# An RWKV-7 chunk recurrence: the inverse multiplied into keys and query products ahead of a two-product chain

## The chip, the cores and the metric

The kernel runs as one program on one core of a Trainium2 chip. The metric is the device time of one execution in microseconds. In the profile the engines are PE (TensorE, matrix products), PEld (its weight loads), DVE (VectorE), ACT (ScalarE), POOL (GpSimd) and SP (SyncE, which issues the DMAs).

## The reference

One block of a streaming encoder with 1024 tokens of 1024 channels: stick-breaking attention and RWKV-7 time mixing run as parallel branches and are merged by gates; a SwiGLU FFN follows. The change lies in the time mixing, whose recurrence is this (8 heads of 64 channels; `state` is one 64x64 matrix for each head):

```python
def wkv7_scan(r, decay, k, v, kk, a):
    ...
    def step(state, inp):
        r_t, w_t, k_t, v_t, kk_t, a_t = inp
        sa = jnp.einsum('bhvk,bhk->bhv', state, -kk_t)
        state = (state * w_t[:, :, None, :]
                 + sa[..., None] * (kk_t * a_t)[:, :, None, :]
                 + v_t[..., None] * k_t[:, :, None, :])
        return state, jnp.einsum('bhvk,bhk->bhv', state, r_t)
    ...
    _, y = lax.scan(chunk_step, state0, tuple(to_chunks(t) for t in (r, decay, k, v, kk, a)))
    return y.reshape(S, B, H, N).transpose(1, 0, 2, 3)
```

All inputs and outputs are float32.

## The kernel before

The kernel first records all operations of the whole block as a list and then orders them: `Block.schedule` plays them through with a cost for each instruction, latencies between engines, a priority (the place in the list plus an offset) and a limited number of buffers for each class of tiles, and `Block.issue` issues every engine's instructions in the order found. Every instruction therefore stands at line 528 of the profile, and instructions are told apart by the names of their tiles. Each engine executes its instructions in that fixed order. A group written under `b.together()` stays in one piece on TensorE.

The time mixing treats heads in four pairs (`PAIRS`), tokens in two halves of 512 (`hf`), and each half in eight chunks of 64 tokens. The two heads of a pair lie on partitions 0 to 63 and 64 to 127. A pair and a half make a unit, eight units in all.

- `rwkv` goes over the pairs: projections of the next pair (`project`, tile class d, 128x512 matmuls), the elementwise work of the two units, gate projections as filler (`gate_tiles`, also class d, 4, 0, 2 and 6 tiles at the four pairs), and the chain of chunks with the highest priority (`CHAIN`).
- `rw_elementwise` prepares for each unit the decayed keys and queries (`xh`, one array per head: the removal key in columns 0 to 63 and the query in 64 to 127 of each chunk), the right operands `bk`, their transposes `bkt` (the keys the state update needs), the values `sv`, centred by a product with a constant 128x128 matrix, and the products of `bk` and `xh`, masked to the triangles within a chunk. The masked products of a head with itself go into `na`, those of the values into the free half of `xh`. Four mask multiplications on VectorE run for each half of four chunks.
- `rw_inverse` inverts the 64x64 triangular matrix of every chunk and head: the 32x32 diagonal blocks by elimination on VectorE (`q` tiles, after a turn through DRAM as `nd` and `td`), then the block below the diagonal by two products of 32x32 tiles on TensorE (names y<-q,na and y<-q,q in the trace). The inverse replaces the masked product in columns 0 to 63 of `na`.
- `rw_chain` steps through the chunks. Each step consists of three groups of products with copies between them:
  1. px: the state and values in `sv` times the removal keys (c<-sv,xa and c<-sv,xb), and with it the state's part of the outputs `y` (y<-xa,sv and y<-xb,sv). VectorE copies px to `xe`.
  2. pu: the inverse times `xe` (c<-xe,na). VectorE copies head 0, ScalarE head 1 into `sv`.
  3. ps: `bkt` times `sv` (c<-sv,bkt), and with it the rest of the outputs (y<-na,sv). Two scalar_tensor_tensor on VectorE, one for each head, form the next state from ps and from the decayed old state `sp`, which GpSimd makes.

  The last chunk of a pair has no ps. Products of single heads are 64 columns wide and are packed: the two heads use different parts of TensorE's array.
- `rw_post` normalizes `y` and stores it.

After the time mixing come `attention`, `merge`, `output` and `ffn`, which the change does not touch.

Of the kernel before, what the change touches and what calls it, by code (L numbers as in the profile page):

```python
# [590 lines left out]
def hybrid_block(tc, x, w_in, consts, params, rows, ups, gup, w_sb, w_rw, w_o, w_fg, w_fu, w_fd, out):  # L591
# [3 lines left out]
    with ExitStack() as es:  # L595
# [9 lines left out]
        b.cls("xe", 3, CH)  # L605
# [207 lines left out]
def rw_elementwise(b, u, p, hf, spill):  # L813
# [76 lines left out]
    for h, q, rs, qs in quads:  # L890
        nc.sync.dma_start(nd[:, 2 * h + q].rearrange("c s t -> s c t"), na[rs, :, qs])
# [13 lines left out]


# [8 lines left out]
    with Offset(b, INV):  # L915
        rw_inverse(b, nd, na, quads, tinit, p, hf)


def rw_inverse(b, nd, na, quads, tinit, p, hf):
# [26 lines left out]
    with b.together():  # L946
        for c, h in ((c, h) for c in range(8) for h in range(2)):
            nc.tensor.matmul(ph[bot[h], c, :], lhsT=na[top[h], c, 32:CH], rhs=dn[top[h], c, :], start=True, stop=True)
    for h in range(2):
# [4 lines left out]
    with b.together():
        for c, h in ((c, h) for c in range(8) for h in range(2)):
            nc.tensor.matmul(pt[top[h], c, :], lhsT=hb[bot[h], c, :], rhs=dt[bot[h], c, :], start=True, stop=True)
    for h in range(2):
        nc.scalar.copy(na[top[h], :, 32:CH], pt[top[h]])


def rw_chain(b, units, p, hf):
# [4 lines left out]
    y = T("y", [P, H])
    u["y"] = y
    hs = [(0, slice(0, CH)), (1, slice(CH, P))]
    for c in range(8):
# [3 lines left out]
        with b.together():
            for h, rs in hs:
                nc.tensor.matmul(px[rs, :], lhsT=xh[h][:, c, 0:CH], rhs=sv[:, c, rs], start=True, stop=True)
            for h, rs in hs:
                nc.tensor.matmul(y[rs, ys], lhsT=sv[:, c, rs], rhs=xh[h][:, c, CH:P], start=c == 0, stop=False, skip_group_check=True)
# [6 lines left out]
        pu = T("c", [P, CH])
        with b.together():
            for h, rs in hs:
                nc.tensor.matmul(pu[rs, :], lhsT=na[rs, c, 0:CH], rhs=xe[rs, :], start=True, stop=True)
        nc.vector.tensor_copy(sv[hs[0][1], c, hs[0][1]], pu[hs[0][1], :])
        nc.scalar.copy(sv[hs[1][1], c, hs[1][1]], pu[hs[1][1], :])
        ps = None if last else T("c", [P, CH])  # L990
        with b.together():
            if not last:
                for h, rs in hs:
                    nc.tensor.matmul(ps[rs, :], lhsT=bkt[:, c, rs], rhs=sv[:, c, rs], start=True, stop=True)
            for h, rs in hs:
                nc.tensor.matmul(y[rs, ys], lhsT=sv[rs, c, rs], rhs=na[rs, c, CH:P], start=False, stop=c == 7, skip_group_check=True)
# [548 lines left out]
```

## Time and profile before

| | us |
|---|---|
| median of 3 runs (1706.15 to 1707.61) | 1707.52 |
| the profiled execution, its own time | 1704.82 |
| span of its instructions | 1702.7 |
| granted TensorE clock, mean | 0.993 |
| TensorE counted busy in the span | 1641.2 |
| VectorE counted busy in the span | 1212.8 |

The first px of the chain starts at 116.6 us, the chain proper at 183.3 (first pu), and its last products at 578.0. In the rows of the prediction an operation stands as out<-in by the names of the tiles: `c_c<-xe_xe,b_na` is a product that writes a tile of class c from xe and na. The number after the names is the part of the array in rows*columns, then the size of the moving operand. In a timeline the first two numbers are the start and the duration in us. In a table by stretch of time each column is the busy time of PE, PEld, DVE, ACT and POOL in the stretch, with the number of instructions, then the granted clock, the share of the DMA engines and GB/s.

### The profile page before, as it was taken

What the parts mean: (1) busy time and instruction counts of PE and PEld (TensorE: products, weight loads), DVE (VectorE), ACT (ScalarE), POOL (GpSimd) and SP (SyncE); (2) the same over time, 40 slices, a digit from 0 to 9 for tenths busy, and PEclk for the clock granted to TensorE, in tenths of its full rate; (3) what the DMA queues carried; (4) which work ended last, traced back from release to release, by engine and by line L of the source; (5) the groups of instructions that cost most, each with busy time, mean ns of one, the idle gap of its engine ahead of it and who ended that gap; (6) DMA issues with size and microseconds to landing.
All of it is one profiled execution on the core that took longest, in us unless ns stands there. A gap on an engine that the chain in (4) does not pass through costs nothing.

```text
span 1702.7 us, 23795 instructions
## 1 busy us (share of the span) xinstructions
PE 1641.2 (96%) x8868; PEld 1267.2 (74%) x8868; DVE 1212.8 (71%) x2167; ACT 712.5 (42%) x1371; POOL 211.1 (12%) x376
## 2 busy tenths in 40 slices
PE   6999999899999989999999999999999999999998
PEld 5777666566666677777778788888888888888886
DVE  6567688989785598898826644866667666777484
ACT  7522233123223476677644443433223233454352
POOL 2031233323313100000003311000000000000000
PEclk9999999899999999999999999999999999999999
DMA  6522222123221000000253721223232333684355
GB/s 228 186 72 94 64 76 82 40 77 101 81 73 57 32 26 13 26 25 26 91 188 106 255 78 44 87 93 118 82 104 93 118 101 105 238 317 136 125 166 180
DMA packets 98147, 178.85 MB, mean 105 GB/s; under 512 B 33392, under 2 KB 34544, under 8 KB 98032
## 3 DMA queue, kind: packets, MB, share of 16 engines
q1 hardware_dynamic: 98032, 177.34, 31.5%
q8 instruction: 70, 1.15, 0.3%
q14 instruction: 45, 0.37, 0.1%
HBM read 129.86 MB, written 47.45 MB: 104 GB/s over the span
## 4 chain that ended last, share of the span: by engine, by line
PE 76%; DVE 17%; ACT 3%; issue 2%; DMA 1%; SPq 0%; DVEq 0%; POOL 0%; ACTq 0%
PE d_d L528 35%; PE e_e L528 16%; PE c_c L528 16%; PE y_y L528 9%; DVE q_q L528 4%; DVE b_nb L528 3%; DVE b_be L528 2%; DVE b_wt L528 1%; DVE wlo_wlo L528 1%; DVE b_na L528 1%; DVE b_bk L528 1%; DVE b_tmp L528 1%; ACT whi_whi L528 0%; DVE b_xb L528 0%; DVE b_xa L528 0%
## 5 line engine op out<-in xcount | busy, mean ns | idle before, releaser
L528 PE MATMUL d_d<-big_h,whi_whi 128*128 128x512 f32 x1280 | 444.1, 413 | 1.9 <-ACT b_sh L528 1.1
L528 PEld LDWEIGHTS d_d<-big_h,whi_whi 128*128 128x128 f32 x1280 | 235.6, 189 | 55.3 <-issue 5.1
L528 PE MATMUL d_d<-big_h,wlo_wlo 128*128 128x512 f32 x640 | 263.4, 412 | 0.0
L528 PEld LDWEIGHTS d_d<-big_h,wlo_wlo 128*128 128x128 f32 x640 | 120.8, 189 | 25.6 <-issue 1.9
L528 ACT CAST whi_whi<-raw_raw 128x1024 fp32r<-128x1024 f32 (+1 forms) x60 | 55.9, 934 | 99.8 <-PE d_d L528 92.5
L528 DVE TENSOR_TENSOR q_q<-b_nl,q_q 128x2 f32<-128x2 f32 (+30 forms) x248 | 86.7, 350 | 9.2 <-PE y_y L528 2.8
L528 DVE TENSOR_TENSOR wlo_wlo<-raw_raw,whi_whi 128x1024 fp32r<-128x1024 f32 (+1 forms) x60 | 70.4, 1175 | 31.0 <-ACT whi_whi L528 30.6
L528 ACT COPY b_sv<-c_c 64x64 f32<-64x64 f32 x64 | 13.3, 207 | 173.6 <-DVE b_sv L528 114.4
L528 DVE TENSOR_TENSOR_SCAN b_nb<-b_nb 128x128 f32<-128x128 f32 (+3 forms) x64 | 85.5, 1352 | 0.6 <-ACT b_nb L528 0.4
L528 POOL TENSOR_SCALAR sp_sp<-b_sv,pl_pl 64x64 f32<-64x64 f32 x120 | 60.2, 502 | 182.3 <-DVE b_sv L528 176.8
L528 DVE TENSOR_REDUCE q_q<-q_q 128x1 f32<-128x2 f32 (+30 forms) x248 | 62.2, 251 | 6.9
L528 PE MATMUL e_e<-b_wd,big_act 128*128 128x512 f32 x264 | 66.6, 395 | 0.0
L528 PE MATMUL d_d<-b_wd,big_act 128*128 128x512 f32 x264 | 66.6, 394 | 0.0
L528 ACT CAST b_wd<-b_wraw 128x512 fp32r<-128x512 f32 x71 | 42.2, 619 | 53.1 <-DVE b_wraw L528 20.7
L528 DVE TENSOR_TENSOR b_wd<-b_wraw,b_wd 128x512 fp32r<-128x512 f32 x71 | 46.7, 686 | 22.8 <-ACT b_wd L528 22.8
L528 PE MATMUL c_c<-cst_cst,b_be 128*128 128x128 f32 x288 | 46.1, 280 | 17.2 <-DVE b_wt L528 11.4
L528 PEld LDWEIGHTS e_e<-b_wd,big_act 128*128 128x128 f32 x264 | 49.6, 188 | 11.8
L528 PEld LDWEIGHTS d_d<-b_wd,big_act 128*128 128x128 f32 x264 | 49.6, 188 | 11.8
L528 PEld LDWEIGHTS c_c<-cst_cst,b_be 128*128 128x128 f32 x288 | 32.1, 140 | 32.3 <-DVE b_wt L528 17.7
L528 ACT CAST b_wt<-c_c 128x512 fp32r<-128x512 f32 (+2 forms) x96 | 43.8, 482 | 21.1 <-PE c_c L528 19.3
L528 DVE TENSOR_TENSOR b_wt<-c_c,b_wt 128x512 fp32r<-128x512 f32 (+2 forms) x96 | 50.1, 547 | 3.2 <-ACT b_wt L528 2.4
L528 PE MATMUL y_y<-b_wd,big_act 128*128 128x512 f32 x198 | 50.5, 394 | 0.0
(609 smaller groups left out, 3742.9 us busy)
## 6 DMA issues: line engine op xcount, KB each, us to landing
raw_raw<-w_in SPq DMA_DIRECT2D x42, 512.0 KB, 3.4
raw_raw<-w_fg SPq DMA_DIRECT2D x22, 512.0 KB, 3.5
raw_raw<-w_fu SPq DMA_DIRECT2D x22, 512.0 KB, 4.1
b_wraw<-w_fd SPq DMA_DIRECT2D x22, 512.0 KB, 5.1
act<-b_u SPq DMA_DIRECT2D x40, 256.0 KB, 3.4
b_x<-x SPq DMA_DIRECT2D x16, 512.0 KB, 6.0
b_mg<-gsc SPq DMA_DIRECT2D x28, 256.0 KB, 5.2
raw_araw<-act SPq DMA_DIRECT2D x14, 512.0 KB, 4.1
```

Source lines behind the costliest of these rows:

```text
L528: getattr(getattr(self.real, op.engine), op.method)(**kw)
```

## The change

The keys and query products that use the inverse are multiplied with it once for each unit, ahead of the chain, so that a step needs no product with the inverse. A step then is one product of the whole 128x128 `sv` with the keys of both heads (`nx`), two copies, and one product of `bkt` with the result `xv`, again for both heads at once. `xv` is a second array beside `sv`, whose value parts come by DMA. The outputs are no longer made in the steps but for four chunks at a time. A unit holds `ar`, `nx` (two tiles), `sv`, `xv`, `bkt` and the half tile `tt`, where it had `xa`, `xb`, `na`, `sv` and `bkt`. The mask multiplications now take all 128 partitions at once.

```diff
@@ rw_elementwise
-    xh = [T("b", [P, 8, P], F32, "xa"), T("b", [P, 8, P], F32, "xb")]
+    ar = T("b", [P, 8, P], F32, "ar")
     bk = T("b", [P, 8 * P], F32, "bk").rearrange("p (c a t) -> p c a t", c=8, a=2)
-    for h, rs in enumerate(halves):
-        nc.vector.scalar_tensor_tensor(out=xh[h][rs, :, 0:CH], in0=c8(kk)[rs], scalar=-1.0, in1=pp[rs, :, 0:CH], op0=ALU.mult, op1=ALU.mult)
-        nc.gpsimd.tensor_tensor(out=xh[h][rs, :, CH:P], in0=c8(r)[rs], in1=pp[rs, :, 1 : CH + 1], op=ALU.mult)
+    nc.vector.scalar_tensor_tensor(out=ar[:, :, 0:CH], in0=c8(kk), scalar=-1.0, in1=pp[:, :, 0:CH], op0=ALU.mult, op1=ALU.mult)
+    nc.gpsimd.tensor_tensor(out=ar[:, :, CH:P], in0=c8(r), in1=pp[:, :, 1 : CH + 1], op=ALU.mult)
...
-        for h, rs in enumerate(halves):
-            for os in halves:
-                dst = na if os is rs else xh[h]
-                nc.vector.tensor_tensor(out=dst[os, c0 : c0 + 4, :], in0=pts[h][os], in1=mask_a[os, None, :].broadcast_to([CH, 4, P]), op=ALU.mult)
+        for h in range(2):
+            nc.vector.tensor_tensor(out=nx[g][:, :, :, h, :], in0=pts[h].rearrange("p c (a t) -> p c a t", a=2), in1=mask2[:, None].broadcast_to([P, 4, 2, CH]), op=ALU.mult)
...
-        nc.sync.dma_start(nd[:, 2 * h + q].rearrange("c s t -> s c t"), na[rs, :, qs])
+        for g in range(2):
+            nc.sync.dma_start(nd[4 * g : 4 * g + 4, 2 * h + q].rearrange("c s t -> s c t"), nx[g][rs, :, 0, h, qs])
...
+    xv = T("b", [P, 8, P], F32, "xv")
+    nc.sync.dma_start(xv[hi, :, lo], sv[hi, :, lo])
+    nc.sync.dma_start(xv[lo, :, hi], sv[lo, :, hi])
...
     with Offset(b, INV):
-        rw_inverse(b, nd, na, quads, tinit, p, hf)
+        tt = rw_inverse(b, nd, nx, quads, tinit, p, hf)
+        for g in range(2):
+            pt = T("y", [P, 4, P])
+            cs = slice(4 * g, 4 * g + 4)
+            with b.together():
+                for c in range(4):
+                    for h, rs in enumerate(halves):
+                        nc.tensor.matmul(pt[rs, c, 0:CH], lhsT=tt[rs, 4 * g + c, :], rhs=bkt[rs, 4 * g + c, rs], start=True, stop=True)
+                    for h, rs in enumerate(halves):
+                        nc.tensor.matmul(pt[rs, c, CH:P], lhsT=tt[rs, 4 * g + c, :], rhs=nx[g][rs, c, 1, h, :], start=True, stop=True)
+            for h, rs in enumerate(halves):
+                nc.scalar.copy(bkt[rs, cs, rs], pt[rs, :, 0:CH])
+                nc.scalar.copy(nx[g][rs, :, 1, h, :], pt[rs, :, CH:P])
+                nc.scalar.copy(nx[g][rs, :, 0, h, :], ar[rs, cs, 0:CH])
@@ rw_chain
-        px = T("c", [P, CH])
...
+        px = T("c", [P, P])
+        nc.tensor.matmul(px, lhsT=nx[c // 4][:, c % 4, 0].rearrange("p h t -> p (h t)"), rhs=sv[:, c, :], start=True, stop=True)
...
...
-        nc.vector.tensor_copy(xe[:], px[:])
...
+        nc.vector.tensor_copy(xv[r0, c, r0], px[r0, r0])
+        nc.scalar.copy(xv[r1, c, r1], px[r1, r1])
         if not last:
+            ps = T("c", [P, P])
+            nc.tensor.matmul(ps, lhsT=bkt[:, c, :], rhs=xv[:, c, :], start=True, stop=True)
...
+        if c % 4 == 3:
...
+            with b.together():
+                for k in range(4 * g, c + 1):
+                    for h, rs in hs:
+                        nc.tensor.matmul(y[rs, k * CH : k * CH + CH], lhsT=sv[rs, k, rs], rhs=ar[rs, k, CH:P], start=k == 0, stop=False, skip_group_check=True)
+                for k in range(4 * g, c + 1):
+                    for h, rs in hs:
+                        nc.tensor.matmul(y[rs, k * CH : k * CH + CH], lhsT=xv[:, k, rs], rhs=nx[g][:, k % 4, 1, h, :], start=False, stop=k == 7, skip_group_check=True)
```

How this moves TensorE's instructions is seen at three places. The first is a chunk step of pair 0 (d is the filler, c the chain, y the outputs). Before, from the second head of px, with the outputs that go along, to pu:

```order
L528 MATMUL c_c_1624<-b_sv_890,b_xb_800 64x64
L528 MATMUL y_y_1053<-b_xa_793,b_sv_890 64x64
L528 MATMUL y_y_1053<-b_xb_800,b_sv_890 64x64
L528 MATMUL d_d_1599<-big_h_169,wlo_wlo_1486 128x512
L528 MATMUL d_d_1599<-big_h_169,whi_whi_1478 128x512
L528 MATMUL d_d_1599<-big_h_175,whi_whi_1478 128x512
L528 MATMUL d_d_1599<-big_h_169,wlo_wlo_1486 128x512
L528 MATMUL d_d_1599<-big_h_169,whi_whi_1478 128x512
L528 MATMUL d_d_1599<-big_h_175,whi_whi_1478 128x512
L528 MATMUL c_c_1644<-xe_xe_1635,b_na_1036 64x64 x2
```

The same place now, from one px to the next:

```order
L528 MATMUL c_c_1652<-b_sv_885,b_nx_1026 128x128
L528 MATMUL d_d_1632<-big_h_169,whi_whi_1407 128x512
L528 MATMUL d_d_1632<-big_h_175,whi_whi_1407 128x512
L528 MATMUL d_d_1632<-big_h_169,wlo_wlo_1415 128x512
L528 MATMUL d_d_1632<-big_h_169,whi_whi_1407 128x512
L528 MATMUL c_c_1665<-b_xv_930,b_bkt_1072 128x128
L528 MATMUL d_d_1632<-big_h_175,whi_whi_1407 128x512
L528 MATMUL d_d_1632<-big_h_169,wlo_wlo_1415 128x512
L528 MATMUL d_d_1632<-big_h_186,whi_whi_1407 128x512
L528 MATMUL d_d_1632<-big_h_195,whi_whi_1407 128x512
L528 MATMUL d_d_1632<-big_h_186,wlo_wlo_1415 128x512
L528 MATMUL c_c_1680<-b_sv_885,b_nx_1026 128x128
```

A step has two single products with four and five filler matmuls behind them, where it had three groups (the third, ps with its outputs, follows after three more filler matmuls).

The second place is new: behind the fourth chunk of the same unit the outputs of four chunks stand in one bundle.

```order
L528 MATMUL c_c_1692<-b_xv_930,b_bkt_1072 128x128
L528 MATMUL y_y_1695<-b_ar_793,b_sv_885 64x64 x8
L528 MATMUL y_y_1695<-b_nx_1026,b_xv_930 64x64 x8
L528 MATMUL d_d_1632<-big_h_195,whi_whi_1407 128x512
L528 MATMUL d_d_1632<-big_h_186,wlo_wlo_1415 128x512
L528 MATMUL c_c_1722<-b_sv_885,b_nx_1054 128x128
```

They stood in each step before.

The third place is the end of the first half of pair 1. Before, steps follow there with no filler between their groups:

```order
L528 MATMUL y_y_2512<-b_xb_1096,b_sv_1900 64x64
L528 MATMUL c_c_2958<-xe_xe_2955,b_na_1967 64x64 x2
L528 MATMUL c_c_2965<-b_sv_1900,b_bkt_2057 64x64 x2
L528 MATMUL y_y_2512<-b_na_1967,b_sv_1900 64x64 x2
L528 MATMUL c_c_2976<-b_sv_1900,b_xa_1085 64x64
L528 MATMUL c_c_2976<-b_sv_1900,b_xb_1096 64x64
L528 MATMUL y_y_2512<-b_xa_1085,b_sv_1900 64x64
L528 MATMUL y_y_2512<-b_xb_1096,b_sv_1900 64x64
L528 MATMUL c_c_2986<-xe_xe_2983,b_na_1967 64x64 x2
```

Now, in the same half, filler stands between them:

```order
L528 MATMUL c_c_2967<-b_sv_1753,b_nx_1901 128x128
L528 MATMUL d_d_2853<-big_h_186,wlo_wlo_2599 128x512
L528 MATMUL d_d_2853<-big_h_186,whi_whi_2572 128x512
L528 MATMUL d_d_2853<-big_h_195,whi_whi_2572 128x512
L528 MATMUL d_d_2853<-big_h_186,wlo_wlo_2599 128x512
L528 MATMUL c_c_2978<-b_xv_1858,b_bkt_1917 128x128
L528 MATMUL d_d_2853<-big_h_186,whi_whi_2572 128x512
L528 MATMUL d_d_2853<-big_h_195,whi_whi_2572 128x512
L528 MATMUL d_d_2853<-big_h_186,wlo_wlo_2599 128x512
L528 MATMUL d_d_2986<-big_h_169,whi_whi_2756 128x512
L528 MATMUL d_d_2986<-big_h_175,whi_whi_2756 128x512
L528 MATMUL c_c_2993<-b_sv_1753,b_nx_1901 128x128
```

The filler of that place stood further behind before, after the products of the next unit.

More of the change, by code (lines that the diff above doesn't have):

```diff
@@ L604, in hybrid_block @@
         b.cls("bf", 2, P)
-        b.cls("xe", 3, CH)
         b.cls("sp", 3, CH)
@@ L871, in rw_elementwise @@
     u["bv"] = bv
-    na = T("b", [P, 8, P], F32, "na")
-    for c0 in (0, 4):
+    mask2 = mask_a.rearrange("p (a t) -> p a t", a=2)
+    nx = [T("b", [P, 4, 2, 2, CH], F32, "nx") for g in range(2)]
+    for g in range(2):
         pts = [T("e", [P, 4, P]) for h in range(2)]
@@ L941, in rw_inverse @@
     nc.vector.transpose(out=dn.rearrange("p c t -> p (c t)"), in_=dt.rearrange("p c t -> p (c t)"))
+    tt = T("b", [P, 8, CH], F32, "tt")
+    for h, q, rs, qs in quads:
+        nc.gpsimd.tensor_copy(tt[rs, :, qs], dn[rs])
+        if q == 0:
+            nc.gpsimd.memset(tt[rs, :, 32:CH], 0.0)
     ph = T("y", [P, 8, 32])
@@ L955, in rw_inverse @@
         for c, h in ((c, h) for c in range(8) for h in range(2)):
-            nc.tensor.matmul(pt[top[h], c, :], lhsT=hb[bot[h], c, :], rhs=dt[bot[h], c, :], start=True, stop=True)
+            nc.tensor.matmul(pt[bot[h], c, :], lhsT=dt[bot[h], c, :], rhs=hb[bot[h], c, :], start=True, stop=True)
     for h in range(2):
-        nc.scalar.copy(na[top[h], :, 32:CH], pt[top[h]])
+        nc.scalar.copy(tt[bot[h], :, 0:32], pt[bot[h]])
+    return tt
 def rw_chain(b, units, p, hf):
@@ L964, in rw_chain @@
     u = units[hf]
-    sv, xh, na, bkt, pl = (u[n] for n in ("sv", "xh", "na", "bkt", "pl"))
-    y = T("y", [P, H])
-    u["y"] = y
+    ar, nx, sv, xv, bkt, pl = (u[n] for n in ("ar", "nx", "sv", "xv", "bkt", "pl"))
     hs = [(0, slice(0, CH)), (1, slice(CH, P))]
+    y = None
     for c in range(8):
         last = hf == 1 and c == 7
-        ys = slice(c * CH, c * CH + CH)
-        px = T("c", [P, CH])
[L973 to L977, printed above, removed]
+        px = T("c", [P, P])
+        nc.tensor.matmul(px, lhsT=nx[c // 4][:, c % 4, 0].rearrange("p h t -> p (h t)"), rhs=sv[:, c, :], start=True, stop=True)
         if not last:
@@ L981, in rw_chain @@
                 nc.gpsimd.tensor_scalar(out=sp[rs, :], in0=sv[rs, c, rs], scalar1=pl[rs, c : c + 1], scalar2=None, op0=ALU.mult)
-        xe = T("xe", [P, CH])
-        nc.vector.tensor_copy(xe[:], px[:])
[L984 to L996, printed above, removed]
+        (_, r0), (_, r1) = hs
+        nc.vector.tensor_copy(xv[r0, c, r0], px[r0, r0])
+        nc.scalar.copy(xv[r1, c, r1], px[r1, r1])
         if not last:
+            ps = T("c", [P, P])
+            nc.tensor.matmul(ps, lhsT=bkt[:, c, :], rhs=xv[:, c, :], start=True, stop=True)
             nsv, ncx = (sv, c + 1) if c < 7 else (units[1]["sv"], 0)
             for h, rs in hs:
-                nc.vector.scalar_tensor_tensor(out=nsv[rs, ncx, rs], in0=ps[rs, :], scalar=pl[rs, c : c + 1], in1=sp[rs, :], op0=ALU.mult, op1=ALU.add)
+                nc.vector.scalar_tensor_tensor(out=nsv[rs, ncx, rs], in0=ps[rs, rs], scalar=pl[rs, c : c + 1], in1=sp[rs, :], op0=ALU.mult, op1=ALU.add)
+        if c % 4 == 3:
+            g = c // 4
+            if y is None:
+                y = u["y"] = T("y", [P, H])
+            with b.together():
[5 more added lines that the diff above has]
+                        nc.tensor.matmul(y[rs, k * CH : k * CH + CH], lhsT=xv[:, k, rs], rhs=nx[g][:, k % 4, 1, h, :], start=False, stop=k == 7, skip_group_check=True)
 def rw_post(b, u, p, hf, spill):
```

12 lines of the change are left out of this document (6 added, 6 removed).

## The prediction

> **What bounds the kernel now.** I read the page's busy times and its chain of work first, then the busy time of the stage that the change touches, and then single instructions on TensorE in order of time.
>
> ```profile
> PE 1641.2 (96%) x8868; PEld 1267.2 (74%) x8868; DVE 1212.8 (71%) x2167; ACT 712.5 (42%) x1371; POOL 211.1 (12%) x376
> PE 76%; DVE 17%; ACT 3%; issue 2%; DMA 1%; SPq 0%; DVEq 0%; POOL 0%; ACTq 0%
> ```
>
> TensorE is counted busy for 96% of the span and holds 76% of the chain that ended last. Busy time overstates it, since matmuls overlap. Starts are the better clock. The recurrence runs from about 184 to 578 us; the first two rows below are the busy time by stretch of all instructions, the third that of the instructions on tile d_d alone (the projections' matmuls, the filler between the chunk steps).
>
> ```profile
> 184.00:578.00 394.00, 378.62 (x2922) 253.48 (x2922) 314.39 (x855) 112.46 (x230) 117.81 (x214) 0.97 0.23 69
> 1300.00:1350.00 50.00, 50.00 (x218) 40.49 (x217) 30.60 (x47) 15.85 (x27) 0.00 (x0) 1.00 0.27 87
> ```
>
> ```profile
> 184.00:578.00 394.00, 269.69 (x902) 156.22 (x900) 15.71 (x22) 30.55 (x47) 0.97 0.23 69
> ```
>
> In the FFN 218 matmuls with 512 columns start in 50 us, 0.229 us each. At that pace the 902 filler matmuls take 207 us of the recurrence's 394. The other 187 us are TensorE's too, counted busy, and go into small products and the turns to and from them. So the stage is bound by TensorE's queue, not by the chain of chunk steps: between the steps there is other work. VectorE comes second (314 of 394).
>
> Where the 187 us go is seen in one chunk (timeline of pair 3; start, duration, engine, operation):
>
> ```profile
> 507.30 0.62 PE L528 MATMUL d_d<-big_h,whi_whi 128*128 128x512 f32 x2
> 507.85 0.33 PE L528 MATMUL c_c<-xe_xe,b_na 64*64 64x64 f32 x4
> 508.11 0.50 PE L528 MATMUL d_d<-big_h,wlo_wlo 128*128 128x512 f32 x1
> 508.25 0.21 ACT L528 COPY b_sv<-c_c 64x64 f32<-64x64 f32 x1 [1.03 <-PE c_c L528]
> 508.45 0.63 PE L528 MATMUL d_d<-big_h,whi_whi 128*128 128x512 f32 x2
> 509.26 0.47 PE L528 MATMUL d_d<-big_h,whi_whi 128*128 128x512 f32 x1 [0.18 <-DVE b_kst L528]
> 509.66 0.34 PE L528 MATMUL c_c<-b_sv,b_bkt 128*64 128x64 f32 x4
> 509.92 0.33 PE L528 MATMUL y_y<-b_na,b_sv 64*64 64x64 f32 x4
> 510.19 0.50 PE L528 MATMUL d_d<-big_h,whi_whi 128*128 128x512 f32 x1
> 510.27 0.59 DVE L528 SCALAR_TENSOR_TENSOR b_sv<-c_c,pl_pl,sp_sp 64x64 f32<-64x64 f32 x2
> 510.52 0.39 PE L528 MATMUL d_d<-big_h,wlo_wlo 128*128 128x512 f32 x1
> 510.75 0.62 PE L528 MATMUL d_d<-big_h,whi_whi 128*128 128x512 f32 x2
> 511.30 0.27 PE L528 MATMUL c_c<-b_sv,b_xa 128*64 128x64 f32 x1
> ...
> 511.68 0.50 PE L528 MATMUL d_d<-big_h,wlo_wlo 128*128 128x512 f32 x1
> 512.02 0.62 PE L528 MATMUL d_d<-big_h,whi_whi 128*128 128x512 f32 x2
> ```
>
> Each float32 product is two matmul instructions, and the two heads' instructions start side by side as a pair. What a group costs is the time it adds between filler matmuls, two of which alone would take 0.46 us:
> - pu (two products, 2 pairs): the second filler of the first row starts at 507.53, and 508.45 is reached after 0.92 us: 0.46 us added.
> - px with its two y products (4 pairs): from 510.98 (one pace after 510.75) to 512.02, 1.04 us: 0.58 added.
> - ps with its two y products: from 509.26 to 510.52, 1.26 us: 0.80 added, of which the longer step into the group (0.40 where the others have 0.32) may be a wait; I take 0.75.
>
> A chunk costs TensorE 0.46 + 0.58 + 0.75 = 1.79 us beside its filler, and 64 chunks 114.6 us. From the first two groups, two pairs more add 0.12 us: a pair is 0.06 and the turn to a packed group and back 0.34. The third has 0.2 more, for the step between two packed shapes (128*64, then 64*64).
>
> **The change, part by part.** *Two whole-array products per chunk* (64 px, 60 ps) replace the three groups. The trace has such a product, 128x128 by 128 columns in float32, in the centring of v: four products, eight instructions.
>
> ```profile
> 144.88 1.02 PE L528 MATMUL d_d<-big_h,whi_whi 128*128 128x512 f32 x2
> 145.74 1.05 PE L528 MATMUL e_e<-cst_cst,b_tmp 128*128 128x128 f32 x8
> 146.55 0.48 PE L528 MATMUL d_d<-big_h,wlo_wlo 128*128 128x512 f32 x1
> 146.86 0.63 PE L528 MATMUL d_d<-big_h,whi_whi 128*128 128x512 f32 x2
> ```
>
> One pace before 145.74 the last filler started (145.51); 146.86 is 1.35 us later, 0.89 more than two fillers: 0.223 us a product and nothing for the turn. 124 of them cost 27.7 us. Bounds: 0.223 from this row, 0.223 + 0.34 from the packed groups, if a lone product between fillers had to pay the turn; I take the first, as the block has the same array shape.
>
> Here a rule is weighed that speaks against this part. The Trainium skill, "TensorEngine Tiling (Array Packing)", Theoretical Speedup, promises up to twice the speed for each dimension of 64 or less that is packed, and the change gives up packing. By its rule alone the new products, whose operands are half zeros or unused, would be the dearer ones; the rows say that streaming is indeed dearer (0.223 against 0.12 for a packed couple), but that the turn decides. Its result is the last rival below.
>
> *The batches.* Per unit (8 units) and half of four chunks, one bundle of 16 products with the inverse (keys and query products), and one of 8 + 8 products for the outputs: 16 bundles of each kind. With 16 pairs the first costs 0.34 + 16 x 0.06 = 1.30 us, the second 0.2 more for its change of shape, 1.50. Together 16 x 2.80 = 44.8 us. No bundle of 64-column products is in the trace; the nearest is that of the masked products, 8 pairs of 128 columns:
>
> ```profile
> 117.84 0.37 PE L528 MATMUL e_e<-b_xa,b_bk 64*128 64x128 f32 x1
> ...
> 118.72 0.27 PE L528 MATMUL e_e<-b_xa,b_bk 64*128 64x128 f32 x1
> ```
>
> Seven steps in 0.88 us are 0.126 a pair. That is the upper bound: 2.36 + 2.56 per half, 78.7 us. I take 0.06, which has the right width. TensorE's sum: 27.7 + 44.8 - 114.6 = **-42 us**; with the upper bound -8.
>
> *VectorE and the other engines.* VectorE loses the copy of px, and half of its mask multiplications (64 instructions over 64 partitions become 32 over 128):
>
> ```profile
> L528 DVE TENSOR_TENSOR b_na<-e_e,cst_cst 64x512 f32<-64x512 f32 x32 | 22.0, 686 | 2.9 <-PE e_e L528 2.3
> L528 DVE COPY xe_xe<-c_c 128x64 f32<-128x64 f32 x64 | 14.3, 224 | 14.7 <-PE c_c L528 13.0
> L528 DVE TENSOR_TENSOR b_xa<-e_e,cst_cst 64x512 f32<-64x512 f32 x16 | 11.1, 694 | 0.4
> L528 DVE TENSOR_TENSOR b_xb<-e_e,cst_cst 64x512 f32<-64x512 f32 x16 | 10.9, 681 | 0.4
> ```
>
> That is 14.3 + 32 x 0.69 = 36 us of 314. As TensorE bounds the stage it counts nothing by itself. ScalarE gets 12 copies of 64x256 a unit, at the duration of its copy into sv:
>
> ```profile
> L528 ACT COPY b_sv<-e_e 64x256 f32<-64x256 f32 x28 | 10.2, 366 | 9.3 <-PE e_e L528 9.0
> ```
>
> 96 x 0.366 = 35 us, beside 282 us in which ScalarE is idle: nothing; uncovered, 4.4 us before a unit's first ps, eight times. The 16 loads of xv copy parts of sv that are written long before the chain, and the transfers for the inverse are split in two: nothing; they would cost their landing only if the chain stood waiting at a unit's start.
>
> *The sparse stretch.* At pair 1 the filler is used up, and the chain waits for VectorE in the open:
>
> ```profile
> 318.00:346.00 28.00, 23.32 (x172) 16.49 (x173) 27.09 (x50) 8.12 (x16) 13.85 (x18) 0.76 0.25 63
> ```
>
> ```profile
> 326.38 0.22 DVE L528 COPY b_sv<-c_c 64x64 f32<-64x64 f32 x1
> 326.65 0.48 PE L528 MATMUL c_c<-b_sv,b_bkt 128*64 128x64 f32 x4 [1.81 <-DVE b_sv L528]
> ```
>
> VectorE is busy for 27.1 of 28 us, TensorE waits up to 1.81 us at a step, and its granted clock is 0.76: 0.24 x 28 = 6.7 us of clock lost. In the new order the steps of pair 1 have four to five filler matmuls between them, and VectorE has less to do. Bounds 0 and -8.5 (the clock and that wait); I take **-6**.
>
> *New waits.* A chunk has two hops now, each with less cover. After px stand four fillers, 0.22 + 0.92 = 1.14 us; needed is 0.40 from a product to its copy (507.85 to 508.25), the copy's 0.21 and a step back, about 0.7. After ps stand five, 1.37 us; needed are 0.40 and the two updates' 0.59, about 1.05. The slack of 0.3 to 0.4 us is less than one mask (0.69). If a tenth of the 124 hops meets such an instruction and loses 0.35, that is **+4**; bounds 0 and 37 (0.3 at every hop).
>
> **Sum:** 1704.8 of the profiled execution (span 1702.7) - 42 - 6 + 4 = 1660.8. The median of the runs shown, 1707.5, is 2.7 above the profiled one; that is within their spread and I leave it out: **1661 us**.
>
> **Rivals.**
> - *Slow bundles:* at 0.126 a pair the gain of TensorE shrinks to 8; with the sparse stretch's 6 and the waits, 1695. For it: these pairs load new weights each time, as the slow bundle does. Against: the width is half.
> - *The hops wait instead:* 0.3 us at every hop, 37 instead of 4: 1694. For it: VectorE is at 80% of the stage and in order. Against: 36 us leave VectorE, and TensorE is the one that is late at most hops now.
> - *More comes back:* the sparse stretch in full (8.5), no new waits, the third group's doubtful 0.05 us was cost and not wait (64 x 0.05 = 3), and TensorE's three waits for an inverse go as well, since VectorE, which computes it, has less in its queue: 42 + 8.5 + 3 + 6.1, 1645. For it, the list of waits in the stage:
>
> ```profile
> PE y_y L528 <- DVE q_q L528: 6.1, 3, 3.2
> ```
>
>   Against: the inverse itself is not shortened.
> - *The turn isn't saved* (ends slower): a lone whole-array product between fillers waits its 0.34 like the packed groups, because the step comes from the semaphore or the change of accumulator and not from the shape. 124 x 0.34 = 42 eats the gain, and with the sparse stretch unchanged and the 4 us of waits it is 1709. It decides from 0.34 on. If nothing of the turns were saved, only the streaming would count: 2 x 0.223 + 8 x 0.06 against 10 x 0.06 a chunk, +0.33 x 64 = 21 us, 1726. Against it: the centring block, which pays nothing. The page of the Trainium skill named above, Theoretical Speedup, would lead one to expect this last case.
>
> **How the numbers follow.** Forecast 0.60, slow bundles 0.12, waiting hops 0.09, more back 0.13, turn not saved 0.06. The range 1640 to 1697 reaches from just below the gain in full to just above the slow bundles, and leaves out the last rival and a little at each end. 0.2% (3.4 us) is about what a measurement of this kernel can tell from no change. Slower by more 0.05, within 0.03, faster 0.92.
>
> **What would show it.** Right: the steps c_c<-b_sv,b_nx and c_c<-b_xv,b_bkt add about 0.22 us between fillers, with no 0.33 us step before them; the bundles take 1.3 to 1.5 us; the recurrence from first to last step is some 44 us shorter, the rest of the span as long as before; granted clock near 1.00 throughout. Wrong: idle time of TensorE before these steps with VectorE or ScalarE as releaser, bundles of over 2 us, or a later stage that gives the time back.

## The result, and the profile after

| | before | after |
|---|---|---|
| median of 4 runs, us | 1707.12 (1706.15 to 1707.61) | 1664.35 (1663.57 to 1664.94) |
| the profiled execution, its own time | 1704.82 | 1664.43 |
| span of its instructions | 1702.7 | 1662.7 |
| granted TensorE clock, mean | 0.993 | 0.998 |
| first step of the chain starts at (pu before, px after) | 183.3 | 168.3 |
| last product of the chain starts at | 578.0 | 534.5 |

The ratio of the times is 0.975, with a 95% interval of 0.9733 to 0.9767: 42.8 us less, where 44 were forecast. The page after, busy times and the shares of the chain that ended last:

```profile
PE 1605.9 (97%) x8876; PEld 1276.6 (77%) x8876; DVE 1163.7 (70%) x2063; ACT 745.5 (45%) x1467; POOL 200.5 (12%) x384
PE 71%; DVE 20%; ACT 3%; issue 3%; DMA 2%; POOL 0%; SPq 0%; DVEq 0%; ACTq 0%
```

TensorE has lost 35 us of busy time, VectorE 49. VectorE's share of the chain has grown from 17% to 20%, TensorE's has fallen from 76% to 71%: the first sign that the waits have moved. The stage of the recurrence by stretch of time, first all instructions, then those on d_d alone:

```profile
160.00:540.00 380.00, 366.64 (x3096) 281.08 (x3096) 278.22 (x778) 153.04 (x339) 112.52 (x227) 0.99 0.29 82
160.00:540.00 380.00, 272.32 (x982) 175.53 (x982) 15.82 (x22) 32.71 (x50) 0.99 0.29 82
```

The 982 filler matmuls at 0.229 us take 225 of 380 us. That leaves 155 for everything else, where before it was 187 of 394.

One chunk of the changed kernel, in order of time (TensorE, VectorE, ScalarE):

```profile
300.52 0.39 PE L528 MATMUL d_d<-big_h,whi_whi 128*128 128x512 f32 x1
300.75 0.38 PE L528 MATMUL c_c<-b_sv,b_nx 128*128 128x128 f32 x2
300.89 0.48 PE L528 MATMUL d_d<-big_h,wlo_wlo 128*128 128x512 f32 x1
301.17 0.22 DVE L528 COPY b_xv<-c_c 64x64 f32<-64x64 f32 x1 [0.72 <-PE c_c L528]
301.21 0.62 PE L528 MATMUL d_d<-big_h,whi_whi 128*128 128x512 f32 x2
301.42 0.21 ACT L528 COPY b_xv<-c_c 64x64 f32<-64x64 f32 x1 [0.63 <-DVE b_xv L528]
301.67 0.39 PE L528 MATMUL d_d<-big_h,wlo_wlo 128*128 128x512 f32 x1
301.90 0.38 PE L528 MATMUL c_c<-b_xv,b_bkt 128*128 128x128 f32 x2
302.04 0.70 PE L528 MATMUL d_d<-big_h,whi_whi 128*128 128x512 f32 x2
302.39 0.68 DVE L528 SCALAR_TENSOR_TENSOR b_sv<-c_c,pl_pl,sp_sp 64x64 f32<-64x64 f32 x2 [1.00 <-PE c_c L528]
302.58 0.40 PE L528 MATMUL d_d<-big_h,wlo_wlo 128*128 128x512 f32 x1
```

From the filler at 300.52 to the second after it, at 301.21, it is 0.69 us, two paces and 0.23: px costs 0.23. From 301.67 to the third filler after it, at 302.58, it is 0.91, three paces and 0.22: ps costs 0.22. There is no 0.33 us step ahead of either. A second thing is in these rows: the two copies of px do not run side by side. ScalarE's starts at 301.42, when VectorE's (301.17, 0.22 us long) has ended, and the profile names VectorE as its releaser. ScalarE's copy ends 0.88 us after px began, the weight load of ps begins 0.05 us later (301.68, on PEld), and px to ps takes 1.15 us here. In the instruction list of the changed kernel the later copy of each of the 64 pairs waits for the engine of the earlier one; in 28 pairs ScalarE's copy is the earlier one. Over the 64 steps the later copy ends 1.29 us after px began (median; 0.88 at the least).

A bundle of outputs behind a ps, TensorE's rows:

```profile
304.44 0.38 PE L528 MATMUL c_c<-b_xv,b_bkt 128*128 128x128 f32 x2
304.76 0.68 PE L528 MATMUL y_y<-b_ar,b_sv 64*64 64x64 f32 x16
305.37 0.69 PE L528 MATMUL y_y<-b_nx,b_xv 128*64 128x64 f32 x16
305.98 0.50 PE L528 MATMUL d_d<-big_h,whi_whi 128*128 128x512 f32 x1
```

32 instructions from 304.76 to 305.98, 1.22 us beside the turns at its ends; with them a bundle adds 1.41 us. The bundle with the inverse adds 1.28.

**Where the time went.** I split the stage in three, for each kernel: the fillers issued up to the last px at 0.229 us each; what the chain's products and the bundles cost without a wait (their number times the time that one of their kind adds between fillers where it doesn't wait; for ps before the median); and the rest, which is the other products, the start of the kernel and all waits. us, up to the last px:

| kernel | time less fillers | chain and bundles | rest |
|---|---|---|---|
| before | 249.1 | 64 x (0.58 + 0.46 + 0.73) = 113.3 | 135.8 |
| after | 210.0 | 124 x 0.23 + 16 x (1.28 + 1.41) = 71.6 | 138.4 |

TensorE's own part has fallen by 41.7 us, and 39.1 arrive. Split at the first step of the chain, the time less fillers falls by 3.3 us ahead of it (62.6 to 59.3) and by 35.8 from there to the last px (186.5 to 150.7). The rest is 2.6 larger, although VectorE has less to do and the sparse stretch is gone:

```profile
318.00:346.00 28.00, 27.08 (x201) 20.21 (x200) 25.35 (x78) 11.94 (x25) 11.01 (x22) 1.00 0.37 106
```

(after; the clock in this stretch was 0.76 before). What has come in are waits at the hops. It shows in what a step adds between fillers. Of the steps that stand alone between fillers, 34 ps add 0.49 us on average and 45 px 0.33, where 0.23 is the price: about 13 us above it in 79 of 124 steps. In the kernel before, 149 groups that stand alone add 4.6 us above their prices (1.8 at pu, 2.1 at ps, 0.7 at px). The releasers of TensorE's weight loads name VectorE and ScalarE (160 to 540 us after; us in total, times, longest):

```profile
PEld c_c L528 <- DVE b_xv L528: 9.2, 17, 1.2
...
PEld c_c L528 <- ACT b_xv L528: 7.2, 13, 1.0
```

By itself this list would not show that waits came in, since a weight load can wait while products run, and the list of before (184 to 578 us) has such waits too:

```profile
PEld c_c L528 <- DVE b_sv L528: 9.1, 17, 2.0
...
PEld c_c L528 <- DVE xe_xe L528: 5.2, 9, 0.8
```

A hop that fails, in order of time:

```profile
398.57 0.49 PE L528 MATMUL c_c<-b_sv,b_nx 128*128 128x128 f32 x2
...
399.20 0.44 DVE L528 TENSOR_TENSOR q_q<-b_nl,q_q 128x150 f32<-128x150 f32 x1
...
399.60 0.40 PE L528 MATMUL d_d<-big_h,whi_whi 128*128 128x512 f32 x1
...
400.02 0.46 DVE L528 TENSOR_TENSOR q_q<-b_nl,q_q 128x182 f32<-128x182 f32 x1
400.51 0.22 DVE L528 COPY b_xv<-c_c 64x64 f32<-64x64 f32 x1
...
400.78 0.38 PE L528 MATMUL c_c<-b_xv,b_bkt 128*128 128x128 f32 x1 [0.78 <-DVE b_xv L528]
```

px starts at 398.57, but the copy of its head 0 comes 1.94 us later, behind instructions of the next inverse in VectorE's queue. The fillers end at 400.0, and TensorE waits for 0.78 us.

### The profile page after: what moved, and what is told of

The parts are those of the page before. It is cut to its first block, busy times and chain, and to the rows that moved or that the text cites. A ratio compares the mean times of both kernels' runs of the same rounds, so it can differ in the third digit from the quotient of the medians.

```text
span 1662.7 us, 23895 instructions
## 1 busy us (share of the span) xinstructions
PE 1605.9 (97%) x8876; PEld 1276.6 (77%) x8876; DVE 1163.7 (70%) x2063; ACT 745.5 (45%) x1467; POOL 200.5 (12%) x384
## 3 DMA queue, kind: packets, MB, share of 16 engines
q8 instruction: 70, 1.15, 0.3%
## 4 chain that ended last, share of the span: by engine, by line
PE 71%; DVE 20%; ACT 3%; issue 3%; DMA 2%; POOL 0%; SPq 0%; DVEq 0%; ACTq 0%
PE d_d L528 30%; PE e_e L528 17%; PE c_c L528 15%; PE y_y L528 9%; DVE q_q L528 7%; DVE b_nb L528 3%; DVE b_be L528 2%; DVE b_wt L528 2%; DVE wlo_wlo L528 1%; DVE b_sv L528 1%; DVE b_nx L528 1%; DVE b_kst L528 0%; ACT b_wt L528 0%; DMA b_b<-rows 0%; DVE b_bk L528 0%
## 5 line engine op out<-in xcount | busy, mean ns | idle before, releaser
L528 PE MATMUL d_d<-big_h,whi_whi 128*128 128x512 f32 x1280 | 435.2, 409 | 3.7 <-DVE b_kst L528 2.8
L528 DVE TENSOR_TENSOR b_wd<-b_wraw,b_wd 128x512 fp32r<-128x512 f32 x71 | 46.7, 686 | 23.6 <-ACT b_wd L528 23.5
L528 ACT COPY b_xv<-c_c 64x64 f32<-64x64 f32 x64 | 13.3, 208 | 91.6 <-DVE b_xv L528 46.2
L528 ACT CAST b_wt<-c_c 128x512 fp32r<-128x512 f32 (+2 forms) x96 | 43.6, 481 | 19.7 <-PE c_c L528 18.0
L528 PE MATMUL c_c<-b_wd,big_act 128*128 128x512 f32 x198 | 50.6, 394 | 0.0
```

What stands on the lines that cost most here:

```text
L528: getattr(getattr(self.real, op.engine), op.method)(**kw)
```

## The experiments

Two questions: does the turn carry the gain, as forecast, or VectorE's relief? And what are the new waits made of? A difference to the changed kernel is that of the two ratios times 1707 us (its ratio is 0.975 [0.9733, 0.9767]); of the kernel before, to 1.

| run | median, us | ratio to before [95%] | difference, us |
|---|---|---|---|
| e1_packed | 1669.83 | 0.9785 [0.9771, 0.9800] | +6.0 to after |
| e2_outputs_each_step | 1680.85 | 0.9846 [0.9830, 0.9862] | +16.4 to after |
| e3_masks_halves | 1686.40 | 0.9889 [0.9869, 0.9909] | +23.7 to after |
| e12_load_beside | 1680.99 | 0.9853 [0.9837, 0.9870] | +17.6 to after |
| e10_inverse_only | 1697.80 | 0.9947 [0.9932, 0.9962] | +33.6 to after, -9.0 to before |
| e6_before_gates | 1702.17 | 0.9976 [0.9964, 0.9988] | -4.1 to before |
| e8_before_load | 1714.66 | 1.0046 [1.0031, 1.0061] | +7.9 to before |
| e9_before_relief | 1700.50 | 0.9967 [0.9954, 0.9980] | -5.6 to before |
| e4_true_costs | 1662.68 | 0.9739 [0.9722, 0.9756] | -1.9 to after |
| e5_serial_costs | 1660.23 | 0.9729 [0.9712, 0.9746] | -3.6 to after |
| e7_copies_scalar | 1662.39 | 0.9736 [0.9720, 0.9752] | -2.4 to after |
| e11_both | 1667.07 | 0.9768 [0.9751, 0.9786] | +3.1 to after |

### The turn: px and ps packed again

```diff
-        px = T("c", [P, P])
-        nc.tensor.matmul(px, lhsT=nx[c // 4][:, c % 4, 0].rearrange("p h t -> p (h t)"), rhs=sv[:, c, :], start=True, stop=True)
+        px = T("c", [P, CH])
+        with b.together():
+            for h, rs in hs:
+                nc.tensor.matmul(px[rs, :], lhsT=nx[c // 4][:, c % 4, 0, h, :], rhs=sv[:, c, rs], start=True, stop=True)
...
```

and ps likewise, with the copies and updates reading px[rs, :] and ps[rs, :].

> The changed kernel, but px and ps are again two packed products of one head each (128 by 64, two pairs of instructions) in place of one whole-array product; all batches stay. Theory of the turn: a packed couple costs 0.34 + 2 x 0.06 = 0.46 us of TensorE's time where the whole-array product costs 0.22, so the 124 steps add 124 x 0.24 = 30 us, less what of the waits at the steps (about 20 us in the changed kernel) hides behind it: 1674 to 1694. Rival, streaming decides (the turn is paid by the whole-array product as well): two pairs stream 0.12 instead of 0.22, 124 x 0.10 = 12 us less: 1652. Rival, the hops bound the steps: no change, 1664.

The time rose by 6 us only: 1669.83 lies below the range of the turn and above both rivals. TensorE's rows show the turn at its full price all the same:

```profile
248.01 0.62 PE L528 MATMUL d_d<-big_h,whi_whi 128*128 128x512 f32 x2
248.56 0.34 PE L528 MATMUL c_c<-b_sv,b_nx 128*64 128x64 f32 x4
248.83 0.50 PE L528 MATMUL d_d<-big_h,wlo_wlo 128*128 128x512 f32 x1
249.16 0.63 PE L528 MATMUL d_d<-big_h,whi_whi 128*128 128x512 f32 x2
```

The second filler of the first row starts at 248.24. To 249.16 it is 0.92, two paces and 0.46, with the 0.32 us step before the group that the whole-array product doesn't have. Chain and bundles cost 124 x 0.46 + 16 x 2.69 = 100.1 us, 28.5 more, but the rest falls from 138.4 to 115.2. At the steps that stand alone the time above the price falls from about 13 to 4 us; where the other 14 us of the rest went is open. Two causes are not told apart here: a step that costs TensorE 0.23 more covers 0.23 more, and the hop itself is shorter (the later copy ends 0.99 us after px began, median, against 1.29). So the price per step in the prediction is right and the streaming rival falls, but at this place most of a saved turn doesn't arrive.

### The outputs in every chunk

```diff
-        if c % 4 == 3:
+        if True:
...
-                for k in range(4 * g, c + 1):
+                for k in (c,):
```

(the last line at both loops)

> The changed kernel, but the outputs are made in every chunk (bundles of 4 + 4 products) in place of once per four chunks (16 + 16 instructions). Theory of the turn: 64 bundles at about 0.34 + 0.2 + 4 x 0.06 = 0.78 us in place of 16 at 1.41, 50 - 23 = +27 us, less what then covers a hop that waits today: 1675 to 1691. Rival, the outputs are cover that the chain needs anyway: within 5 us of the changed kernel, 1659 to 1669.

+16.4 us, in the range of the turn. TensorE's rows of one ps with its outputs:

```profile
302.64 0.63 PE L528 MATMUL d_d<-big_h,whi_whi 128*128 128x512 f32 x2
303.10 0.38 PE L528 MATMUL c_c<-b_xv,b_bkt 128*128 128x128 f32 x2
303.41 0.33 PE L528 MATMUL y_y<-b_ar,b_sv 64*64 64x64 f32 x4
303.68 0.34 PE L528 MATMUL y_y<-b_nx,b_xv 128*64 128x64 f32 x4
303.94 0.50 PE L528 MATMUL d_d<-big_h,wlo_wlo 128*128 128x512 f32 x1
304.27 0.62 PE L528 MATMUL d_d<-big_h,whi_whi 128*128 128x512 f32 x2
```

From the second filler at 302.87 to 304.27, less two paces, it is 0.94: 0.72 for four pairs of outputs, where a share of the large bundle costs 1.41 / 4 = 0.35. Chain and bundles rise by 64 x 0.72 - 16 x 1.41 = 23.5 us, and the rest falls by 4. Batching the outputs is the part of the change whose saving on TensorE arrives best: the cover that the small bundles would give behind each ps is worth 4 us only.

### VectorE: the masks in halves, a load beside the path, and the same in the kernel before

Four runs. In e3_masks_halves each mask multiplication runs over 64 partitions twice:

```diff
-            nc.vector.tensor_tensor(out=nx[g][:, :, :, h, :], in0=pts[h].rearrange("p c (a t) -> p c a t", a=2), in1=mask2[:, None].broadcast_to([P, 4, 2, CH]), op=ALU.mult)
+            for os in halves:
+                nc.vector.tensor_tensor(out=nx[g][os, :, :, h, :], in0=pts[h].rearrange("p c (a t) -> p c a t", a=2)[os], in1=mask2[os, None].broadcast_to([CH, 4, 2, CH]), op=ALU.mult)
```

> The changed kernel, but each mask multiplication over 128 partitions is again two over 64, 64 instructions of about 0.69 us in place of 32: VectorE has 22 us more to do in the recurrence. Theory that TensorE's queue bounds and VectorE's relief counted nothing: 1664 to 1669 (a little more waiting at the hops). Rival, VectorE's relief was a good part of the gain: +10 to +22 us, 1675 to 1687.

In e12_load_beside the real masks stay as they are, and 32 more run behind them into a tile that nothing reads:

```diff
+        for h in range(2):
+            jk = T("jk", [P, 4, 112])
+            nc.vector.tensor_tensor(out=jk[:], in0=pts[h][:, :, 0:112], in1=mask_a[:, None, 0:112].broadcast_to([P, 4, 112]), op=ALU.mult)
```

> The changed kernel with 32 mask multiplications more (128 partitions by 448, about 0.6 us each, 19 us together), behind the real ones, into a tile that nothing reads. It tells VectorE's load apart from the length of the path through the masks: the halved masks cost 22 us and had both. Theory of the load (VectorE's queue delays the copies and updates of the hops): 12 to 20 us more, 1676 to 1684. Rival, the path through the masks to the inverse is what cost: 1664 to 1670.

The groups of these instructions, in the changed kernel, in e3 and in e12 (instructions, then busy us and mean ns of one):

```profile
L528 DVE TENSOR_TENSOR b_nx<-e_e,cst_cst 128x512 f32<-128x512 f32 x32 | 21.3, 683 | 1.6 <-PE e_e L528 1.2
```

```profile
L528 DVE TENSOR_TENSOR b_nx<-e_e,cst_cst 64x512 f32<-64x512 f32 x64 | 44.0, 687 | 3.2 <-PE e_e L528 1.8
```

```profile
L528 DVE TENSOR_TENSOR jk_jk<-e_e,cst_cst 128x448 f32<-128x448 f32 x32 | 19.7, 617 | 0.2
```

22.7 us of VectorE cost 23.7 us of time; 19.7 us whose result nobody reads cost 17.6. So load on VectorE's queue counts even outside the masks: in the changed kernel a microsecond of it is worth about 0.9 (0.7 to 1.2 by the intervals of the two runs). My own expectation for e3 (0 to 5 us) falls, and with it the sentence that VectorE counts nothing. Load and path are not wholly apart in e12, though. The added instructions stand in VectorE's one queue ahead of the inverse, and the first step of the chain starts at 177.0 us in e3 and in e12, where it was 168.3; 8 of the 32 even ran ahead of the masks that they follow in the program. By the profiled runs 1.6 of e12's 16 us are lost ahead of the first step, 9.8 from there to the last px and 4.7 behind it (time less fillers). How the load reaches TensorE is seen in e3 ahead of the chain:

```profile
146.75 1.22 DVE L528 TENSOR_TENSOR wlo_wlo<-raw_raw,whi_whi 128x1024 fp32r<-128x1024 f32 x1
147.88 0.46 DVE L528 TENSOR_TENSOR q_q<-b_nl,q_q 128x182 f32<-128x182 f32 x1
148.25 0.74 DVE L528 SCALAR_TENSOR_TENSOR b_upw<-d_d,small_small,b_cum 128x512 f32<-128x512 f32 x1
...
149.05 0.80 PE L528 MATMUL d_d<-big_h,whi_whi 128*128 128x512 f32 x1 [4.17 <-DVE b_upw L528]
```

The filler itself waits for 4.2 us, for a d tile that VectorE reads last, behind the inverse in its queue. Fillers cover a hop only as long as VectorE empties their tiles.

The same question to the kernel before: e8_before_load splits half of its mask multiplications by partitions (32 instructions more, 32 x 0.69 = 22 us), e9_before_relief gives the 64 copies of px into xe (14.3 us) to ScalarE.

```diff
-                nc.vector.tensor_tensor(out=dst[os, c0 : c0 + 4, :], in0=pts[h][os], in1=mask_a[os, None, :].broadcast_to([CH, 4, P]), op=ALU.mult)
+                for q in (0, 1) if os is rs else (2,):
+                    ps = slice(os.start + 32 * q, os.start + 32 * q + 32) if q < 2 else os
+                    nc.vector.tensor_tensor(out=dst[ps, c0 : c0 + 4, :], in0=pts[h][ps], in1=mask_a[ps, None, :].broadcast_to([ps.stop - ps.start, 4, P]), op=ALU.mult)
```

```diff
-        nc.vector.tensor_copy(xe[:], px[:])
+        nc.scalar.copy(xe[:], px[:])
```

> The kernel before, but half of its mask multiplications (32 of 64) are split in two again, by partitions: 32 more instructions of about 0.69 us, VectorE has 22 us more to do. The same load that cost the changed kernel 22 us. By the prediction (TensorE's queue bounds this stage, VectorE counts nothing): 1706 to 1712. Rival, VectorE is a bound of the kernel before as well: 1720 to 1729.

> The kernel before, but the copy of px into xe (64 copies, 14.3 us) is ScalarE's, where it was VectorE's; nothing else is changed. It asks what VectorE's relief alone was worth. By the prediction (VectorE counts nothing here): 1703 to 1709. Rival, VectorE's load is part of what bounds the stage: 8 to 14 us less, 1693 to 1699.

+7.9 for 22 us more, -5.6 for 14.3 less: 0.36 and 0.39 a microsecond (0.24 to 0.55 by their intervals), between the two theories. VectorE was a partial bound before as well, and with TensorE's part 42 us smaller it is nearly a full one. The profiled run of e8, 9.9 us longer than that of the kernel before, shows where the price is paid. From first pu to last px the chain is 23.6 us longer, but TensorE fills that with 101 more fillers: the time less fillers grows by 3.0 us ahead of the first pu and by 0.4 in the chain. The other 6.5 us are lost behind it, where 114 fillers fewer are left.

### What is left without the three

e10_inverse_only is the edits of e1, e2 and e3 together.

> The changed kernel with three of its parts undone together: px and ps packed per head, outputs in every chunk, masks in 64-partition halves. What is left of the change is the inverse multiplied in ahead of the chain (no pu, no xe, two hops per chunk). By durations, TensorE then has (0.46 + 0.73) x 64 = 76 us in the chain and 16 x 1.28 = 20 in the bundles, 96 where the kernel before has 113; VectorE has 14 us less than before. Alone the three cost 5.5, 16.5 and 22 us. If they add up: 1664 + 44 = 1708, no faster than the kernel before, and the inverse's batch would be worth nothing alone. Theory that a step's time goes to TensorE or to a wait at the hop but not to both, so that the three cover each other: 1685 to 1698.

1697.80, at the upper end of the last range: 9.0 us faster than before, and 33.6 above the changed kernel, where the three alone sum to 46: they cover each other in part. My price for TensorE there was too low: a packed ps with its own outputs adds 0.99 us, not 0.73, so that chain and bundles cost 64 x (0.46 + 0.99) + 16 x 1.28 = 113, as much as before. By that sum the 9 us are not TensorE's products. They need not be the inverse's batch either, as two more things are left in e10. The removal keys are made by 8 instructions over 128 partitions, where 16 over 64 made them (6.1 us of VectorE for 13.4), and the sparse stretch of the kernel before is filled, at a clock of 1.00 where it was 0.76:

```profile
318.00:346.00 28.00, 27.47 (x301) 19.08 (x299) 20.20 (x38) 12.49 (x31) 12.77 (x24) 1.00 0.25 67
```

Estimates from the other runs, the missing xe copies at 14.3 x 0.38 = 5, the removal keys at 7.3 x 0.38 = 3 and the stretch at e6's 4, already reach 12 us. Nothing is left that has to be the missing hop; it was not tried apart.

### The sparse stretch alone

```diff
-GATES_R = (4, 0, 2, 6)
+GATES_R = (4, 2, 2, 4)
```

in the kernel before.

> The kernel before, with its gates of filler (4, 0, 2, 6) changed to (4, 2, 2, 4), so that pair 1 gets filler of the later pairs; nothing of the change itself is in it. It prices the sparse stretch by itself. If that stretch cost about 13 to 15 us (its waits and 13.65 us of half clock, as the comparison of the two traces suggests): 1693 to 1697 for a kernel that was 1707. By the term of the prediction (6 us, at most 8.5): 1699 to 1701. Rival, the filler only moves and another stretch goes sparse instead: 1705 to 1709.

The stretch is filled, and TensorE's clock is at 1.00 where it was 0.76:

```profile
318.00:346.00 28.00, 27.78 (x188) 18.41 (x188) 24.30 (x53) 8.37 (x15) 5.53 (x13) 1.00 0.34 93
```

4.1 us, near the forecast's 6. The 13 to 15 us that I had read from the two traces, from its waits and its half clock, was too much. Part of that time seems to come back elsewhere: in e6 TensorE is busy for 13.3 of the 16 us from 400 to 416, where it was 15.2, and its clock from 500 to 520 is 0.91, where it was 1.00.

### Can the new waits be bought off?

Four runs. e4_true_costs and e5_serial_costs change only the planner's costs of the chain's 64x64 operations, so that more filler stands behind each product (e5 has 460.0 for the copies):

```diff
+    if n == CH and out.shape[0] == CH and engine in ("vector", "scalar"):
+        return 300.0 if method == "scalar_tensor_tensor" else 215.0
```

> The changed kernel, but the planner is told the measured durations of the chain's 64x64 operations (copies 0.215 us, updates 0.30 us), so that it puts one filler matmul more behind each chain product (five and six where four and five stand). Theory that the hops are short of cover (about 20 us of waits at the steps, a copy that begins only when the other head's copy has ended): one filler more is 0.23 us of cover against waits of 0.26 and 0.10 us a step, 5 to 15 us less: 1649 to 1659. Rival, the waits come from wide VectorE instructions ahead of the copies, which no filler of 0.23 covers, or the time is only moved: 1661 to 1667.

> The changed kernel, but the planner is told 0.46 us for each head's copy (two copies one after the other) and 0.30 us for an update, so that five to seven fillers stand behind px and six behind ps. Theory that uncovered hops cost about 20 us: 10 to 20 us less, 1644 to 1654, unless the filler runs out before the last pair and a sparse stretch takes some of it back. Rival, the time is only moved: 1661 to 1667. Rival, filler runs out early: slower than 1667, with an idle TensorE late in the recurrence.

e7_copies_scalar gives both copies to ScalarE; e11_both is e7 with the costs of e4.

```diff
-        nc.vector.tensor_copy(xv[r0, c, r0], px[r0, r0])
+        nc.scalar.copy(xv[r0, c, r0], px[r0, r0])
```

> The changed kernel, but both copies of px into xv are ScalarE's, where one was VectorE's: VectorE has 64 x 0.22 = 14 us less to do, ScalarE as much more, and the second copy, which today starts when the other engine's has ended, still comes second. Theory from the run with split masks (22 us more of VectorE's work cost 22 us): VectorE's load decides, 10 to 14 us less: 1650 to 1655. Rival, the hops decide by their own length, which stays as it is: 1661 to 1667. Rival, ScalarE's queue delays the copies: over 1667.

> The changed kernel with both copies of px on ScalarE and the planner told the chain's measured durations (copies 0.215 us, updates 0.30 us): 64 x 0.22 us off VectorE, and a filler matmul more behind ps, whose updates waited longer when the copies alone were moved. The two edits gave 2 and 1.7 us apart. Theory that the waits at both hops are one supply of time: 1654 to 1660. Rival, filler spent in the chain is missing in the attention stage behind it: 1660 to 1664.

All four intervals overlap that of the changed kernel, so none is shown to beat it, and none reaches the range of its own theory. In e5 the waits at lone ps fall from 9.1 to 0.7 us, and the time less fillers at the last px from 210.0 to 197.0, 13 us: the hop waits are real and can be covered. But 131 fillers more are used up in the chain, and behind it the time less all matmuls on tile d grows by 738.6 us to the end, where it was 731.4: 7 us of the 13 are given back behind the chain, where those fillers are missing. In e7 ps hardly waits any more, and px does, for the state's updates (matmul waits in the stage, e7 and then the changed kernel):

```profile
PE c_c L528 <- DVE b_sv L528: 6.6, 14, 0.9
```

```profile
PE c_c L528 <- DVE b_sv L528: 0.6, 1, 0.6
```

14 us off VectorE gave 2.4 us, within the two intervals, though 20 us on it cost 17.6. The waits moved from one hop to the other: above a price of 0.22 the lone ps fall from 9.1 to 0.6 us, and the lone px rise from 4.8 to 13.7. Why the updates come later with less in VectorE's queue is not explained by these runs. e11, which gave ps a filler more, left the time less fillers at the last px where e7 has it (207.5 and 208.1 us).

## Why the prediction was right

Point by point, by its own steps:

- **Whole-array products without a turn, 0.223 us:** right, 0.23 and 0.22. e1 shows the price of the packed alternative, 0.46, exactly as the sum 0.34 + 2 x 0.06 has it. The rival "turn isn't saved" falls.
- **Bundles 1.30 and 1.50:** right, 1.28 and 1.41. The rival "slow bundles" falls.
- **TensorE's sum -42:** right as a sum of its products, 113.3 to 71.6, -41.7. Whether it arrives is another matter: e1 shows that 28.5 us of TensorE's work put back at the steps cost 6, e2 that 23.5 us put back behind ps cost 16.
- **VectorE's 36 us count nothing:** wrong. This is the step that failed. The argument was that TensorE's queue bounds the stage and VectorE is second. But VectorE's microseconds were worth 0.36 to 0.39 before (e8, e9) and 0.9 to 1.0 after (e3, e12). The relief was also larger than 36 us: VectorE is counted busy for 49 us less, and the removal keys, which the sum left out, are 7.3 of them. 44 us (14.3 + 22 + 7.3) at 0.38 are an estimated 17 us, if one takes VectorE's relief first; the runs give no single share, since the worth depends on what else has been changed.
- **New waits +4:** mis-sized. In the 79 lone steps alone there are about 13 us. The cover was counted rightly (1.15 us from px to ps in the chunk above, against 1.14), but what is needed was put at 0.7 us, as if the two copies ran side by side; they run one after the other, and the later one ends 1.29 us after px began (median), before the weights of ps can be loaded. The bound of 37 was not reached. One of the prediction's own signs of being wrong, TensorE waiting before these steps for VectorE or ScalarE, is there. "The hops wait instead" was half right as a mechanism and wrong as the result.
- **Sparse stretch -6:** about right; filled in the kernel before it was worth 4.1, and the clock came back as forecast.
- **Loads of xv, ScalarE's 96 copies:** not tried apart. Neither of them is among the larger waits of the stage.
- **The rest of the span as long as before:** right. From the last product of the chain to the end it is 1128.2 us after and 1124.7 before, with 21 more fillers in it, 4.8 us.
- **The recurrence some 44 us shorter:** only at its end, where the last product starts 43.5 us earlier. From first step to last product it is 366.2 us, where it was 394.7: 28.5 less. The other 15 us are an earlier start, of which TensorE's time less fillers shows 3.3.

So the change came out within 1.2 us by the medians (42.8 where 44 were forecast) and within 3.6 by the profiled runs (40.4), because two errors are opposite: waits at the hops that were left too small (by some 9 us), and a relief of VectorE that was left out (an estimated 17). The terms as measured or estimated (-41.7 of products, -4.1, +13 and -17) sum to -50 and not to -40: they cover each other, and the runs give no share for each. The prices of TensorE's products were right; that the total came so close is luck. The two belong together in part: e3 and e12 show that with a longer queue on VectorE the same short steps lose 18 to 24 us.

## What to carry to other kernels

A busy share of 96% on one engine and 80% on another, in order and feeding each other several times per step, can be two bounds and not one, as it was here: price a saving on either by putting a known load on it (a dead instruction of 0.6 us, 32 times) and seeing how much of it arrives. Group small packed products in long bundles and keep lone products in the filler's array shape; each change of shape cost 0.2 to 0.34 us here, for products of 0.06 us. Of TensorE's time saved that way the bundled outputs kept 16 of 23.5 us, the lone px and ps only 6 of 28.5. When a step loses work on the bounding engine, subtract the cover that this work gave to the next hop, and read the hop's length from the trace with its copies in the order in which they really run.

## What the runs showed of the hardware

- In the changed kernel, VectorE and GpSimd side by side:

```profile
383.15 1.29 POOL L528 TENSOR_TENSOR b_tmp<-b_sh,b_tmp 128x512 f32<-128x512 f32 x1 [0.77 <-DVE q_q L528]
383.31 0.28 DVE L528 SCALAR_TENSOR_TENSOR b_sv<-c_c,pl_pl,sp_sp 64x64 f32<-64x64 f32 x1 [0.20 <-PE c_c L528]
383.51 1.01 DVE L528 TENSOR_TENSOR q_q<-b_nl,q_q 128x56 f32<-128x56 f32 x1
...
384.55 0.29 DVE L528 SCALAR_TENSOR_TENSOR b_sv<-c_c,pl_pl,sp_sp 64x64 f32<-64x64 f32 x1
...
384.99 0.35 PE L528 MATMUL c_c<-b_sv,b_nx 128*128 128x128 f32 x1 [0.62 <-DVE b_sv L528]
```

  The multiplication at 383.51, whose like takes 0.25 us elsewhere, ends 0.08 us after GpSimd's has, and head 1's update and the next px wait behind it. The update at 383.31, which reads a product's tile (c) and one array, is not held up. Of the 248 such multiplications of the inverse 11 are more than 1.3 times their shortest, 5.4 us together, 9 of them beside a tensor_tensor of GpSimd. The Trainium skill, "SBUF — State Buffer", SBUF: two separate sides, says that VectorE's instructions with two inputs in SBUF and GpSimd's that read it share a pair of ports, one at a time, for the whole instruction; the trace agrees, and no run here took GpSimd's work away.
- A change of array shape costs 0.2 to 0.34 us, and a whole-array product between whole-array products none: 0.46 against 0.23 for the same two heads' work (e1 and the changed kernel).
- The mask multiplications take the same 0.68 us over 64 partitions (e3) as over 128 (the changed kernel).
